# A hybrid decoder layer on one core: a plainer entry to the second feed-forward, held-back gate columns, a spread spatial-gating norm and later operand loads

## The chip, the cores and the metric

The kernel runs on one NeuronCore of a Trainium2 chip. The number that counts is device time in microseconds (us) of one execution. Before the change the median of three runs is 2202.64 us (2201.89 to 2203.19). The engines are named as the profile names them: PE is the matrix engine (TensorE), PEld its weight loads, DVE the vector engine, ACT the scalar engine, POOL GpSimd, SP the sync engine, whose queue issues the transfers spoken of here.

## The reference

One inference step of one decoder layer, for 1024 prompt tokens and 32 sample tokens (8 sequences of 4) that share the weights; D = 1024, feed-forward width 2816.

```python
h = layer_norm(ALPHA * x + 0.5 * swiglu(x, f1_w1, f1_w3, f1_w2), ln1_g, ln1_b)      # FFN-a
z = h @ w_in + b_in                       # 2304 for q, k, v; 1024 for u, v; 2048 for two gates
att = combine_groups(outs, lses)          # 3 groups of 4 heads, windowed and dilated attention
yb, vrows = sgu_branch(uv, sgu_ln_g, sgu_ln_b, sgu_ws, sgu_b)     # u * (tril(ws) @ LN(v) + b)
mix = (jax.nn.sigmoid(ga) * (att @ w_oa) + jax.nn.sigmoid(gb) * (yb @ w_ob)) @ w_out
h = layer_norm(ALPHA * h + mix, ln2_g, ln2_b)                                       # LN2
h = layer_norm(ALPHA * h + 0.5 * swiglu(h, f2_w1, f2_w3, f2_w2), ln3_g, ln3_b)      # FFN-b, LN3
```

Returned besides `h` are the key and value windows of both token kinds and `vrows`, the normalised v rows of the sample tokens (`svo` in the kernel). All is float32.

## The kernel before

**Layout.** Activations lie transposed, features on 128 partitions and the 1056 tokens along the free axis, cut into four column chunks of C = 264 (NC = 4). Every float32 operand is split into a rounded high part and a rest (`split`, L236 to L240: a cast on ACT at L238, a subtraction on DVE at L239), and a product takes three matmuls (`mm3`, L227): high by high, low by high, high by low. A dense 128-feature by 264-token product over 1024 inputs (`dense8`) is 24 such matmuls of 128x128 by 128x264. Feed-forward blocks go through a Strassen-like scheme (seven products of 24 matmuls, 168, for what takes 192 plainly); the blocks named in `PLAIN` can be done plainly by column chunk with `hidden8` (L405 to L419), which needs only the chunk's normalised columns.

**Stages.** FFN-a, the wide projection `w_in`, the mix (attention, spatial gating, gates, the three output products), then FFN-b. `gate8` (L944 to L956) computes one 128-feature block of z for one chunk on PE, evicts it on ACT (L954) and stores it to `zD` in DRAM (L955). `fetch_z` (L1102) loads a block of z back; `fetch_qkv` loads the three blocks that a step of attention needs.

**Mix.** `attend` (L1120 to L1233) runs six times, as a generator: per step V transposes (L1144), scores (L1164), mask and maximum on DVE (L1172), exponentials on ACT (L1176), turn transposes (L1187) copied by ACT (L1191), values (L1203), and a last transpose of maxima and sums (L1225), copied by DVE (L1227) and stored to `mlD` (L1229). The combination generator (L1235 to L1292) reads `mlD` in a [16, ...] form (L1247 to L1253), forms the weights of the three groups, stores them to `cD` (L1276), loads them broadcast over partitions (L1283) and scales the attention rows on DVE (L1288 to L1291). `sgu_norm` (L1402 to L1456) transposes the v blocks (L1433, copied at L1435), takes their statistics on DVE, the root on ACT and DVE (`rsqrt`, L628 to L634), and normalises with nine passes on ACT (L1447). `sgu_mix` (L1458 to L1487) makes `yb`. `mix` (L1489 to L1635) interleaves these with dense work: the last z blocks, then per output block n the product with w_ob (`local(n)`), which multiplies the gate tile `mt[n]` in place (L1505), and the product with w_oa, which is scaled by the gate tile `ta[n]` and added to it; the sum is split and feeds w_out.

**LN and FFN-b.** `norm` (L580 to L626) is a generator per chunk: sums of squares by ones-matmuls (L589), the root on ACT and DVE, a broadcast by matmul (L597), scaling on DVE (L608), affine on ACT (L616) or DVE (L613). In `ffn` (L641 to L721), block 0 of FFN-b is done chunk by chunk as LN2's chunks become ready; the spread sums (`s1`) that Strassen needs follow after chunk 3.

**What sets the order.** The file is a program of generators (`bg`, `mid`, `slow`) that dense work ticks by counted steps; a scheduler then sets each engine's order of instructions by simulated time and by the tile pools: 37 slots S, 8 weight tiles W, 6 mid tiles M, 2 raw tiles R, and the matmul banks mm (3) and ax (5). All transfers that are spoken of go through SP in the order written. An engine executes strictly in its order, so an instruction that waits holds all behind it.

Of the kernel before, what the change touches and what calls it, by code (L numbers as in the profile page):

```python
# [13 lines left out]
F32R = mybir.dt.float32r  # L14
AF = mybir.ActivationFunctionType
# [49 lines left out]
WARM = 2  # L65
FENCED = (mybir.EngineType.DVE, mybir.EngineType.Activation, mybir.EngineType.SP)
# [4 lines left out]
LAST = 4  # L71
EARLY = 6
# [7 lines left out]
class Trunk:  # L80
# [131 lines left out]
    def unit(self, src, n=D, slot=False, ahead=URGENT):  # L212
        new = self.S if slot else self.W
        with self.tc.high_priority(offset=ahead):
            raw = self.R([P, D])
            hi, lo = new([P, D], F32R), new([P, D], F32R)
            dma = self.nc.sync.dma_start(raw[:, :n], src[:, :n])
            self.split(hi[:, :n], lo[:, :n], raw[:, :n])
        self.fence[mybir.EngineType.SP] = dma.ins
# [362 lines left out]
    def norm(self, c, i, mode, Y, s):  # L582
# [7 lines left out]
        r, t = self.X([P, 3], "rs"), self.X([P, 3], "rt")  # L590
        self.rsqrt(r, t, pv, EPL)
# [35 lines left out]

    def rsqrt(self, r, t, v, eps):  # L628
# [12 lines left out]
    def ffn(self, w13, w2p, w2, i, mode, resid):  # L641
        nc, preps = self.nc, {}
        last = FB + NG * (KB // 2) - 1
# [27 lines left out]
        else:  # L671
# [3 lines left out]
            self.step(self.bg, 1)  # L675
            begin(1)
            for c in range(NC):
                self.drain(lns.pop(c))
                self.hidden8(units, 0, c)
                if c:  # L680
                    with self.chained():
                        next(preps[1], None)
            self.bg.append(s1)
# [5 lines left out]
        def ready(f):  # L689
            for _ in preps.pop(f):  # L690
                pass
            if f < last:
                begin(f + 1)

        def between(f, bg, slow=0):
            if f + 1 in preps:
                next(preps[f + 1], None)
# [8 lines left out]
        for f in range(1, FB):  # L706
# [5 lines left out]
            def after():  # L712
# [4 lines left out]
            self.hidden(f, after)  # L717
# [400 lines left out]
    def attend(self, i):  # L1118
# [19 lines left out]
        self.fetch_qkv(i + 1)  # L1138
# [77 lines left out]
        for t in range(6):  # L1216
# [4 lines left out]
            if t < 4:  # L1221
                scores(t)
            yield from self.pause(SPREAD)
# [12 lines left out]
    def combine(self, hp):  # L1236
# [3 lines left out]
        for g in range(3):  # L1240
            x = raw[:, g]
            for m in range(2):
                for h in range(2):
                    src = self.mlD[hp, g, m, h]
                    o = x[8 * h : 8 * h + 8, m]
                    if g == 0:
                        nc.sync.dma_start(o, src.rearrange("(a x) -> a x", a=8))  # L1247
                    elif g == 1:
                        nc.sync.dma_start(
                            o.rearrange("p (r b) -> p r b", r=4), src.rearrange("(r a b) -> a r b", r=4, a=8)  # L1250
                        )
                    else:
                        nc.sync.dma_start(  # L1253
                            o.rearrange("p (r b) -> p r b", r=16), src.rearrange("(r a b) -> a r b", r=16, a=8)
# [25 lines left out]
        cbs = [self.S([P, NP]) for _ in range(3)]  # L1280
        for g, cb in enumerate(cbs):
            for h in range(2):
                nc.sync.dma_start(cb[64 * h : 64 * h + 64], self.cD[hp, g, h].partition_broadcast(64))  # L1283
        yield from self.pause(3)
        for g, cb in enumerate(cbs):
            aT = self.attT.pop((hp, g))
# [113 lines left out]
    def sgu_norm(self):  # L1400
# [28 lines left out]
        for i in range(9):  # L1429
# [19 lines left out]
        v = self.M([NS, 512])  # L1449
        for op, k in ((ALU.mult, "sgu_ln_g"), (ALU.add, "sgu_ln_b")):  # L1450
            t = self.M([NS, 512])
            nc.sync.dma_start(t, a[k].partition_broadcast(NS))
            nc.vector.tensor_tensor(v, vn[4][:NS, 0] if op == ALU.mult else v, t, op=op)
        nc.sync.dma_start(a["svo"], v)
        self.vn = vn
# [32 lines left out]
    def mix(self):  # L1488
# [18 lines left out]
        def local(n):  # L1507
            wb = self.unit(a["wo"][n, :, 2 * P :], 4 * P)
# [12 lines left out]
        sgu = [self.sgu_norm()] + [self.sgu_mix(gg) for gg in range(4)]  # L1521
# [7 lines left out]
        for c in range(NC):  # L1529
# [4 lines left out]
            for n in units:  # L1534
                self.gate8(units[n], DENSE[n], c, AF.Identity, STEPS["tail"], 1)
        units = self.A = None
        while any(g in self.mid for g in sgu):
            self.step(self.mid, 1)
        def column_sums():
# [254 lines left out]
```

## Time and profile before

| what | value |
|---|---|
| median of three runs | 2202.64 us |
| profiled execution, its own time | 2200.98 us |
| its span (first to last instruction) | 2199.2 us |
| mean granted PE clock | 0.988 |
| PE, DVE, ACT, POOL busy in the span | 97%, 71%, 41%, 15% |
| chain that ended last | PE 81%, DMA 7%, DVE 7%, ACT 2% |

The profiled execution stands 1.66 us under the median, so a saving found in its trace is taken from the median without rescaling. Of the span, 1.8 us lie outside of it. The windows that matter are 1076 to 1330 us (attention beside spatial gating and gates), 1300 to 1400 (the end of attention, w_ob, w_oa and w_out), 1490 to 1550 (LN2 and the entry to FFN-b) and the last 20 us (LN3). In a row of a timeline stand the start, the length of the group, the engine, the line, the operation, out<-in and the count; in square brackets the idle time ahead of the group and what ended it. In a row of windows stand busy times and counts of PE, PEld, DVE, ACT and POOL, then the granted clock of PE, the share of the DMA engines and GB/s.

### The profile page before, as it was taken

The page shows a single profiled execution, that of the slowest core. Times are in us where ns is not written, and L with a number is a line of the kernel's source. Part 1 is how long each engine was busy: PE and PEld are TensorE (multiplying, and loading weights), DVE is VectorE, ACT ScalarE, POOL GpSimd, SP SyncE. Part 2 cuts the span into 40 slices and gives each one's busy share as a digit, 9 for nine tenths or more (in the row PEclk, how much of TensorE's full clock was granted, in tenths as well). Part 3 has the DMA queues.
Part 4 walks back from the last instruction along what each step waited for, and adds up shares of the span by engine and source line. Part 5 has one row for each costly group of instructions (what it writes and reads, how often), then busy time and mean ns, then how long its engine had stood idle before and what let it go on. Part 6 is the DMA issues. An engine that isn't in the chain of part 4 may idle for free.

```text
span 2199.2 us, 43234 instructions
## 1 busy us (share of the span) xinstructions
PE 2133.2 (97%) x17281; PEld 2092.9 (95%) x17281; DVE 1564.8 (71%) x2718; ACT 898.1 (41%) x1690; POOL 330.1 (15%) x238
## 2 busy tenths in 40 slices
PE   9999999999998999999989998998999999999997
PEld 8999999999998999999879897998999999999997
DVE  8777776656788725887674648778676776657787
ACT  5444444421225634344465354246444444322224
POOL 0432332200010022232000000000432332100000
PEclk9999999999999999999989999999999999999999
DMA  4435545598873325666854547513445545596751
GB/s 157 146 134 177 179 161 177 193 367 324 330 279 136 135 102 188 215 215 221 313 165 152 172 156 245 187 51 126 165 158 178 171 161 185 186 384 264 295 192 79
DMA packets 170553, 429.82 MB, mean 195 GB/s; under 512 B 24864, under 2 KB 61456, under 8 KB 167664
## 3 DMA queue, kind: packets, MB, share of 16 engines
q1 hardware_dynamic: 169920, 426.53, 55.3%
q8 instruction: 135, 2.21, 0.4%
q10 hardware_dynamic: 432, 0.54, 0.1%
q14 instruction: 66, 0.54, 0.1%
HBM read 305.97 MB, written 167.22 MB: 215 GB/s over the span
## 4 chain that ended last, share of the span: by engine, by line
PE 81%; DMA 7%; DVE 7%; ACT 2%; issue 1%; POOL 1%; SPq 1%; ACTq 0%; DVEq 0%; POOLq 0%
PE ax L227 43%; PE mm L227 35%; DMA M<-kv 4%; DVE W L239 1%; PE ax L1164 1%; DMA zD<-M 1%; DMA S<-zD 1%; PE ax L1203 1%; DVE S L239 1%; PE ax L1187 1%; DMA R<-wz 0%; DVE X L1346 0%; DVE S L608 0%; DVE X L1361 0%; DVE M L1345 0%
## 5 line engine op out<-in xcount | busy, mean ns | idle before, releaser
L227 PE MATMUL ax<-S,W 128*128 128x264 f32 x5472 | 716.2, 284 | 0.8 <-ACT S L994 0.5
L227 PE MATMUL mm<-S,W 128*128 128x264 f32 x5040 | 677.4, 289 | 25.8 <-DVE S L1505 9.3
L227 PEld LDWEIGHTS ax<-S,W 128*128 128x128 f32 x5472 | 685.6, 188 | 3.3 <-ACT S L994 1.5
L227 PEld LDWEIGHTS mm<-S,W 128*128 128x128 f32 x5040 | 641.6, 191 | 43.1 <-issue 10.7
L227 PE MATMUL ax<-S,S 128*128 128x264 f32 x3288 | 483.7, 285 | 2.9 <-DVE S L1003 2.8
L227 PEld LDWEIGHTS ax<-S,S 128*128 128x128 f32 x3288 | 434.2, 188 | 4.1 <-DVE S L1003 4.1
L227 PE MATMUL mm<-S,S 128*128 128x264 f32 x2496 | 388.4, 286 | 9.0 <-ACT S L238 4.0
L227 PEld LDWEIGHTS mm<-S,S 128*128 128x128 f32 x2496 | 337.7, 189 | 11.5 <-ACT S L238 4.4
L238 ACT CAST W<-R 128x256 fp32r<-128x256 f32 (+2 forms) x172 | 127.6, 759 | 316.8 <-PE mm L227 118.2
L369 POOL TENSOR_TENSOR Q<-R 128x512 f32<-128x512 f32 x50 | 72.1, 1443 | 793.1 <-DMA R<-w13b 217.1
L239 DVE TENSOR_TENSOR W<-R,W 128x256 fp32r<-128x256 f32 (+2 forms) x172 | 152.6, 891 | 28.2 <-ACT W L238 24.0
L238 ACT CAST W<-Q 128x1024 fp32r<-128x1024 f32 (+1 forms) x79 | 77.9, 986 | 217.1 <-POOL Q L370 91.7
L780 DVE SCALAR_TENSOR_TENSOR S<-ax,S 128x264 f32<-128x264 f32 x240 | 99.9, 431 | 69.6 <-PE ax L227 68.5
L444 DVE TENSOR_TENSOR S<-ax,M 128x264 f32<-128x264 f32 x84 | 33.7, 433 | 150.6 <-PE ax L227 150.6
L106 POOL CAST S<-ones 128x1 fp32r<-128x1 f32 x32 | 18.3, 594 | 745.5 <-PE mm L227 663.8
L239 DVE TENSOR_TENSOR S<-Q,S 128x1024 fp32r<-128x1024 f32 (+1 forms) x79 | 111.8, 1415 | 3.5 <-ACT S L238 3.3
L239 DVE TENSOR_TENSOR W<-Q,W 128x1024 fp32r<-128x1024 f32 (+1 forms) x79 | 92.0, 1164 | 24.5 <-ACT W L238 24.5
L238 ACT CAST S<-Q 128x1024 fp32r<-128x1024 f32 (+1 forms) x79 | 77.8, 985 | 74.1 <-PE ax L227 55.0
L238 ACT CAST S<-R 128x512 fp32r<-128x512 f32 (+1 forms) x65 | 44.6, 686 | 116.5 <-DMA sumsA<-S 42.6
L239 DVE TENSOR_TENSOR S<-S,M 128x528 fp32r<-128x528 f32 x72 | 85.6, 1189 | 2.1 <-ACT M L238 0.2
L370 POOL TENSOR_TENSOR Q<-Q,R 128x512 f32<-128x512 f32 x50 | 83.6, 1673 | 2.7
L377 POOL TENSOR_TENSOR Q<-R,Q 128x512 f32<-128x512 f32 x50 | 82.7, 1653 | 1.2
(199 smaller groups left out, 2063.3 us busy)
## 6 DMA issues: line engine op xcount, KB each, us to landing
ws<-st SPq DMA_DIRECT2D x144, 256.0 KB
S<-sumsA SPq DMA_DIRECT2D x63, 528.0 KB
S<-sumsB SPq DMA_DIRECT2D x63, 528.0 KB
M<-kv SPq DMA_DIRECT2D x96, 256.0 KB
sumsA<-M SPq DMA_DIRECT2D x90, 264.0 KB
sumsB<-M SPq DMA_DIRECT2D x90, 264.0 KB
R<-w13b SPq DMA_DIRECT2D x44, 512.0 KB
S<-zD SPq DMA_DIRECT2D x42, 528.0 KB
```

What stands on the lines that cost most here:

```text
L106: self.nc.gpsimd.tensor_copy(t[:, 0, :1] if len(shape) == 3 else t[:, :1], self.ones[:, :1])
L227: mm = lambda a, b, s, e: nc.tensor.matmul(o, a[:, cc], b, start=s, stop=e, skip_group_check=True)
L238: a = self.nc.scalar.copy(hi, src)
L239: b = self.nc.vector.tensor_tensor(lo, src, hi.bitcast(F32), op=ALU.subtract)
L369: tt(s12[:, lo], cd[:, lo], cd[:, hi], op=ALU.add)
L370: tt(s12[:, hi], s12[:, lo], ab[:, lo], op=ALU.subtract)
L377: tt(s34[:, hi], ab[:, hi], s12[:, hi], op=ALU.subtract)
L444: go(one, 5, False, lambda x: tt(h[:, x, 1], one[x], p7[:, x], op=ALU.add))
L780: nc.vector.scalar_tensor_tensor(y(x, r, e), bank[x], HALF, y(x, r, e), op0=ALU.mult, op1=ALU.add)
L1164: nc.tensor.matmul(pS[h][:, r, :nk], q[e, i * P : (i + 1) * P], k[e, k0 : k0 + nk], start=True, stop=True)
L1187: nc.tensor.transpose(pT[r][:, h, o], s[:, r, h, o], self.ident)
L1203: nc.tensor.matmul(pv[0][e, (i % 4) * P : (i % 4 + 1) * P], V[:, i - (nb - 1) + b, e], sT[:, r, h, b * P : b * P + P], start=b == 0, stop= ...
```

## The change

Five things are changed; line numbers move by some 12 to 60 in the new file.

1. FFN-b starts with two plain blocks, 0 and 19, each done chunk by chunk behind LN2 (FFN-a keeps one); the spread sums `s1` are queued ahead of the last chunk. Block 19 is left out of the later Strassen blocks.
2. The last gate units, three now (four before), are computed for chunks 0 to 2 only; their chunk 3 is done by `beside` after the w_oa blocks 2, 4 and 5. All eight w_ob blocks stand before the end of attention (six before). Their weights, and those of w_oa, take one W tile (`narrow`), and `ta` is fetched three blocks ahead.
3. `sgu_norm` takes its root on DVE (`rsqrt_dve`: an integer start and three Newton steps, eleven small instructions) and pauses two steps between transposes; the stored sample rows are a generator of their own at the end of the list.
4. LN2's last chunk and LN3's third chunk take their root on DVE; one Silu activation on a single column follows LN2's third chunk.
5. `fetch_qkv` of the next step moves from the start of a step to its `t == 3`; the combination reads `mlD` of group 0 with one transfer, and loads the three broadcast tiles one after another.

```diff
@@ narrow (new)
+    def narrow(self, src, n):
+        with self.tc.high_priority(offset=URGENT):
+            raw = self.R([P, D])
+            both = self.W([P, D], F32R)
+            hi, lo = both[:, :n], both[:, n : 2 * n]
+            dma = self.nc.sync.dma_start(raw[:, :n], src)
+            self.split(hi, lo, raw[:, :n])
...
@@ norm
+        if c == NC - 1 and i == 1 or c == NC - 2 and mode == "out":
+            self.rsqrt_dve(r, t, self.X([P, 3], "rx", 1), pv, EPL)
+        else:
+            self.rsqrt(r, t, pv, EPL)
+        if i == 1 and c == NC - 2:
+            nc.scalar.activation(self.X([P, 2], "warm", 1)[:, :1], r[:, :1], AF.Silu)
...
+    def rsqrt_dve(self, r, t, x, v, eps):
+        nc = self.nc
+        tt = nc.vector.scalar_tensor_tensor
+        nc.vector.tensor_scalar(x, v, eps, None, op0=ALU.add)
+        nc.vector.tensor_scalar(r.bitcast(I32), x.bitcast(I32), -0.5, MAGIC, op0=ALU.mult, op1=ALU.add)
+        for _ in range(3):
+            nc.vector.tensor_tensor(t, x, r, op=ALU.mult)
+            tt(t, t, -0.5, r, op0=ALU.mult, op1=ALU.mult)
+            self.chain = tt(r, t, 1.5, r, op0=ALU.add, op1=ALU.mult).ins
@@ ffn
+        plain = PLAIN[: 1 if i == 0 else 2]
+        blocks = [f for f in range(FB) if f not in plain] + [FB + g for g in range(NG * (KB // 2))]
...
+            lead = [units] + [[self.unit(w13[f, x]) for x in range(2)] for f in plain[1:]]
             begin(1)
             for c in range(NC):
                 self.drain(lns.pop(c))
-                self.hidden8(units, 0, c)
...
-            self.bg.append(s1)
+                if c == NC - 1:
+                    self.bg.append(s1)
+                    self.step(self.bg, 2)
+                for f, u in zip(plain, lead):
+                    self.hidden8(u, f, c)
...
@@ attend
-        self.fetch_qkv(i + 1)
+        follower = i + 1
...
+            if t == 3:
+                self.fetch_qkv(follower)
             yield from self.pause(SPREAD)
@@ combine
+            if g == 0:
+                nc.sync.dma_start(x, src.rearrange("m h (a x) -> (h a) m x", a=8))
...
+        load(0)
+        load(1)
         yield from self.pause(3)
-        for g, cb in enumerate(cbs):
+        for g in range(3):
+            load(g + 2)
...
@@ sgu_norm
-            yield
+            yield from self.pause(2)
...
-        self.rsqrt(rs[:, 0], rs[:, 1], mv[:, :, 1], EPS)
+        self.rsqrt_dve(rs[:, 0], rs[:, 1], mv[:, :, 1], mv[:, :, 1], EPS)
...
@@ mix
-            wb = self.unit(a["wo"][n, :, 2 * P :], 4 * P)
+            wb = self.narrow(a["wo"][n, :, 2 * P :], 4 * P)
...
-            for n in units:
-                self.gate8(units[n], DENSE[n], c, AF.Identity, STEPS["tail"], 1)
-        units = self.A = None
+            if c < NC - 1:
+                for n in units:
+                    self.gate8(units[n], DENSE[n], c, AF.Identity, STEPS["tail"], 1)
...
+        def beside(n):
+            m = DENSE[n] - 26
+            p = self.mm_tile()[:, :C]
+            self.dense8(p, units.pop(n), NC - 1)
+            with self.urgent():
+                nc.scalar.activation(ta[m][:, -C:], p, AF.Identity, bias=self.bin(DENSE[n]))
...
-        for n in range(EARLY):
+        for n in range(KB):
             local(n)
-        ta = [self.fetch_z(26 + n) for n in range(2)]
+        self.yb = None
+        ta = [fetch_gate(n) for n in range(3)]
...
-            wa = self.unit(a["wo"][n], 2 * P)
-            if n + 2 < KB:
-                ta.append(self.fetch_z(28 + n))
-            if n < KB - EARLY:
-                local(EARLY + n)
+            wa = self.narrow(a["wo"][n, :, : 2 * P], 2 * P)
+            if n + 3 < KB:
+                ta.append(fetch_gate(n + 3))
...
+            if n in BESIDE:
+                beside(BESIDE[n])
```

Where the order of the engines moves is shown at three places. The first is ACT at the spatial-gating norm, beside the second step of attention: the table load and root of `sgu_norm`, the nine normalising passes, and the exponentials of the attention step. Before:

```order
L630 ACT_TABLE_LOAD
L630 ACTIVATE X_13274<-X_12957,eps_163 128x9
L1145 COPY Q_13366<-ax_13367 128x512
L1210 COPY S_12932<-ax_13231 128x512
L1145 COPY Q_13366<-ax_13373 128x512
L1447 ACTIVATE S_12952<-S_12952,X_13274 128x512 x2
L1447 ACTIVATE S_12953<-S_12953,X_13274 128x512 x2
L1447 ACTIVATE S_12954<-S_12954,X_13274 128x512 x2
L1447 ACTIVATE S_12955<-S_12955,X_13274 128x512 x2
L1447 ACTIVATE S_12956<-S_12956,X_13274 32x512
L1176 ACT_TABLE_LOAD
L1176 ACTIVATE S_13415,X_13413<-S_13415,X_13413 128x128
```

After, where L1212 are the exponentials, L990 the evictions of `gate8`, L1227 the copies of the turn and L1489 the nine passes:

```order
L1212 ACTIVATE S_13390,X_13388<-S_13390,X_13388 128x128
L1212 ACTIVATE S_13390,X_13388<-S_13390,X_13388 128x256
L990 ACTIVATE M_13639<-mm_13614,cols 128x264
L1227 COPY S_13413<-ax_13406 128x512
L1227 COPY S_13413<-ax_13405 128x2x128
L1489 ACTIVATE S_12942<-S_12942,X_13434 128x512 x2
L1489 ACTIVATE S_12943<-S_12943,X_13434 128x512 x2
L1489 ACTIVATE S_12944<-S_12944,X_13434 128x512 x2
L1489 ACTIVATE S_12945<-S_12945,X_13434 128x512 x2
L1489 ACTIVATE S_12946<-S_12946,X_13434 32x512
L990 ACTIVATE M_13680<-mm_13655,cols 128x264
L1212 ACTIVATE S_13416,X_13388<-S_13416,X_13388 128x128
```

The two table loads are gone, and the nine passes stand behind the first turn of the step instead of ahead of its first exponentials.

The second place is SP at the end of attention. In the names, zD is z in DRAM, mlD and cD the tables of the combination; L1102 before and L1138 after are `fetch_z`, here the tiles `mt[4]` and following. Before:

```order
L1102 DMA S_15245<-zD_8669 128x1056
L1102 DMA S_15247<-zD_8670 128x1056
L1229 DMA mlD<-X_15237 32x128
L1247 DMA S_15282<-mlD 8x128 x4
L1249 DMA S_15282<-mlD 8x4x32 x4
L1253 DMA S_15282<-mlD 8x16x8 x4
```

After:

```order
L1311 DMA cD<-S_15276 16x128 x3
L1321 DMA S_15306<-cD 64x1024 x2
L1321 DMA S_15309<-cD 64x1024
L1138 DMA S_15312<-zD_8666 128x1056
L1138 DMA S_15314<-zD_8667 128x1056
L1138 DMA S_15322<-zD_8668 128x1056
L1321 DMA S_15309<-cD 64x1024
L1321 DMA S_15344<-cD 64x1024
L1138 DMA S_15412<-zD_8669 128x1056
```

Blocks zD_8669 and zD_8670 (`mt[4]`, `mt[5]` before; the numbering of zD differs by three between the files, so that these are zD_8666 and zD_8667 after) stood ahead of the store to `mlD` and stand behind the store to `cD` now.

The third place is ACT at the entry to FFN-b, where L415 and L428 evict a gate of block 0, L616 and L635 are LN2's affine passes. Before, with two changes of table and back around the root of chunk 3 (L630):

```order
L328 CAST S_17454<-S_17413 128x1056
L415 ACT_TABLE_LOAD
L415 ACTIVATE M_17638<-mm_17588 128x264
L238 CAST S_17150<-S_16387 128x1056
L328 CAST S_17488<-S_17456 128x1056
L328 CAST S_17522<-S_17411 128x1056
L328 CAST S_17554<-S_17490 128x1056
L630 ACT_TABLE_LOAD
L630 ACTIVATE X_17571<-ax_17567,eps_165 128x3
L415 ACT_TABLE_LOAD
L415 ACTIVATE M_17714<-mm_17664 128x264
```

After, where the loads are gone from this stretch (the one that remains, at L610, stands ten rows ahead of the first of these):

```order
L341 CAST S_17426<-S_17385 128x1056
L428 ACTIVATE M_17630<-mm_17580 128x264
L251 CAST W_17576<-R_17570 128x1024
L251 CAST S_17122<-S_16360 128x1056
L341 CAST S_17460<-S_17428 128x1056
L341 CAST S_17494<-S_17383 128x1056
L341 CAST S_17526<-S_17462 128x1056
L428 ACTIVATE M_17706<-mm_17656 128x264
L428 ACTIVATE M_17760<-mm_17710 128x264
```

The first evictions of block 0 and block 19 follow one another, with no root of chunk 3 on ACT between them.

More of the change, by code (lines that the diff above doesn't have):

```diff
@@ L704, in load @@
                     loads.popleft()()
-        for f in range(1, FB):
+        for f in blocks[: FB - len(plain)]:
             ready(f)
@@ L710, in ffn, with step @@
             count = iter(range(1, 8))
-            def after():
+            def step():
                 between(f, STEPS["strassen"])
@@ L715, in after @@
                     load(min(HEAD, 2 + 4 * next(count)))
-            self.hidden(f, after)
+            self.hidden(f, step)
             del self.L[f]
```

82 lines of the change are left out of this document (47 added, 35 removed).

## The prediction

> **What bounds the kernel now.** I read the windows first, to see where PE is not busy.
>
> ```profile
> 1100.00:1150.00 50.00, 42.52 (x356) 36.84 (x355) 35.30 (x96) 33.12 (x81) 0.00 (x0) 0.90 0.55 168
> 1150.00:1200.00 50.00, 48.45 (x379) 43.65 (x379) 26.00 (x86) 27.98 (x83) 0.00 (x0) 0.93 0.48 157
> ...
> 1300.00:1350.00 50.00, 44.31 (x345) 42.35 (x345) 34.96 (x84) 19.21 (x40) 0.00 (x0) 0.93 0.61 195
> 1350.00:1400.00 50.00, 43.08 (x321) 40.76 (x321) 45.16 (x70) 19.86 (x23) 2.66 (x6) 0.97 0.79 284
> ...
> 1500.00:1550.00 50.00, 45.11 (x347) 44.17 (x347) 41.13 (x55) 25.53 (x39) 8.13 (x6) 0.93 0.37 125
> 1550.00:1600.00 50.00, 50.00 (x413) 50.00 (x412) 33.52 (x49) 22.02 (x38) 16.83 (x12) 1.00 0.50 171
> ```
>
> The last row is a window in which PE is the bound: 413 matmuls in 50 us, 0.121 us each; there only fewer matmuls help. The others lose time twice, by idle PE and by a granted clock under 1. I count a window's loss as 50 minus busy, plus busy times (1 minus clock). 1100 to 1200 loses 7.5 + 4.3 + 1.6 + 3.4 = 16.7 us; 1300 to 1400 loses 5.7 + 3.1 + 6.9 + 1.3 = 17.0 us. For 1500 to 1550 the count does it: 413 - 347 = 66 matmuls, 8.0 us. These 42 us are nearly all that the change can win. The list of PE's waits says for whom PE waits (total, times, longest):
>
> ```profile
> PE ax L1187 <- ACT S L1176: 10.0, 4, 5.9
> PE mm L227 <- DVE S L1505: 9.3, 9, 3.2
> PE mm L227 <- ACT S L238: 8.8, 3, 4.0
> PE mm L227 <- ACT M L415: 2.7, 3, 1.9
> ...
> PE ax L1144 <- DMA S<-zD: 1.3, 1, 1.3
> ```
>
> The first is attention behind ACT, the second w_ob and w_oa behind DVE's gate products, the third and fourth mostly the entry to FFN-b; the last is part 3's. The timeline shows each.
>
> **Part 1: plain entry to FFN-b.** Block 19 takes 192 matmuls instead of 168: 24 by 0.121 = **+2.9 us**, certain, since PE is the bound in this stage. What it can win is the entry's loss (the first row is part 4's):
>
> ```profile
> 1336.15 4.19 PE L227 MATMUL mm<-S,W 128*128 128x264 f32 x21 [3.18 <-DVE S L1505]
> ...
> 1493.94 2.83 PE L227 MATMUL mm<-S,S 128*128 128x264 f32 x21 [1.87 <-ACT M L415]
> ...
> 1504.15 0.73 PE L597 MATMUL ax<-ident,X 128*128 128x128 f32 x6
> ...
> 1511.91 0.81 PE L227 MATMUL mm<-S,S 128*128 128x264 f32 x2 [4.02 <-ACT S L238]
> 1512.52 1.74 PE L227 MATMUL mm<-S,W 128*128 128x264 f32 x7
> ```
> ```profile
> 1492.20 1.28 ACT L415 ACT_TABLE_LOAD   x1
> ...
> 1497.79 1.28 ACT L630 ACT_TABLE_LOAD   x1
> ...
> 1499.37 1.28 ACT L415 ACT_TABLE_LOAD   x1
> ```
>
> The 1.87 us wait is an eviction behind the first of these table loads; the warm-up activation moves that load ahead, and the root of chunk 3 on DVE takes the other two away. The 4.02 us wait is for LN2's chunk 3, whose split on ACT is late, and the matmuls behind it run at 1.74/7 = 0.25 us each. After the change, about 130 dense matmuls (15.7 us) lie on PE between the broadcast of chunk 3's root and the first matmul that reads chunk 3; before, 24 (2.9 us). From that broadcast to the first matmul PE took from 1504.15 to 1511.91, 7.8 us, and 15.7 us of cover is twice that. Loss taken away: 8.0 + 1.9 = 9.9 us. Late next is block 19's second weight: its rest comes from a raw tile that is cast and subtracted when ACT is full of LN2. As nearest row I take the first wait above, behind ACT in the same crowd, and leave 1.9 us (bounds 0, all hidden, and 5.9, the longest wait of the list). Net of it −8.0, with the matmuls **−5.1 us** (−7.0 to −1.1).
>
> [...] The 0.25 us behind the 4.02 us wait agree with half clock. [...]
>
> **Part 2: spatial gating.** Before, ACT does the root and nine passes in one piece, and PE waits for the exponentials behind them:
>
> ```profile
> 1119.93 1.28 ACT L630 ACT_TABLE_LOAD   x1
> ...
> 1124.34 6.46 ACT L1447 ACTIVATE S<-S,X 128x512 f32<-128x512 f32 x9 [0.27 <-DVE X L1443]
> 1130.82 1.28 ACT L1176 ACT_TABLE_LOAD   x1
> 1132.12 0.40 ACT L1176 ACTIVATE S<-S,X 128x128 f32<-128x128 f32 x1
> ```
> ```profile
> 2182.95 0.17 DVE L631 RECIPROCAL X<-X 128x3 f32<-128x3 f32 x1
> ...
> 2184.08 0.16 DVE L634 SCALAR_TENSOR_TENSOR X<-X,X 128x3 f32<-128x3 f32 x1
> ```
> ```profile
> 1134.98 1.54 PE L1187 MATMUL ax<-ident,S 128*128 128x128 f32 x6 [5.88 <-ACT S L1176]
> ...
> 1139.51 3.74 PE L227 MATMUL mm<-S,W 128*128 128x264 f32 x22
> ...
> 1149.81 0.88 PE L1187 MATMUL ax<-ident,S 128*128 128x128 f32 x6 [1.15 <-ACT S L1176]
> 1151.86 2.73 PE L1164 MATMUL ax<-S,S 64*128 64x128 f32 x8 [1.18 <-DVE M L1483]
> ```
>
> The root on DVE is eleven instructions. Of the four that DVE does now, the row in the middle shows those of LN3, 0.16 us each; with other work between they start up to 0.4 us apart. At 0.2 us eleven are 2.2 us, on an engine that was busy 35.30 of 50 us: hidden, as nobody but the nine passes waits for it. Two table loads, 2.6 us, go from ACT. The nine passes still take 6.46 us in one piece, but they stand behind a turn's copies, with some 60 dense matmuls (7.3 us) on PE ahead of the next turn. What is late next: three turns, score groups and values follow with no dense work between, since all three matmul banks wait for an eviction on ACT. By the old waits at the same places (1.15, 1.18, and half of 5.88) I leave 5.3 us idle and half of the 7.7 us lost to clock. From 16.7 us that is 9.2 left, −7.5; because pauses push the gating back toward the end of attention I take **−6.0 us** (−12 to 0).
>
> **Part 3: operands later.** `fetch_qkv` moves from a step's start to its fourth turn, on SP behind what stands there:
>
> ```profile
> 1124.93 6.97 SPq L1330 DMA_DIRECT2D M<-kv  x6
> ...
> 1327.11 1.05 SPq L1102 DMA_DIRECT2D S<-zD  x2
> ...
> 1333.85 1.08 ACT L1513 ACTIVATE S<-S 128x1056 f32<-128x1056 f32 x1 [2.29 <-DMA S<-zD]
> ```
>
> Six slabs of the sample caches hold the queue 7 us, and a block of z took 6.7 us from issue to its first reader. Between the moved loads and the first V transposes PE has 6 to 9 us of work in the new order. So each of five steps may wait between 0 and 6.7 us; what waits behind a V transpose is all of PE. PE waited only once for such a load before, 1.3 us. I take 0.8 us each, **+4.0 us** (0 to 33). It buys slots S for other tiles, whose worth no row shows: nothing.
>
> **Part 4: gate columns held back, w_ob first.** The 72 matmuls of three units' chunk 3 and the order of w_ob leave 78 fewer dense matmuls ahead of the end of attention: 9.4 us earlier, and the work comes back behind it, where PE idled (3.18 us at 1336.15, and then):
>
> ```profile
> 1309.29 0.27 PE L1225 MATMUL ax<-ident,X 128*32 128x128 f32 x1
> ...
> 1342.60 1.01 PE L227 MATMUL mm<-S,W 128*128 128x264 f32 x3 [2.26 <-ACT S L238]
> ...
> 1383.42 35.68 PE L227 MATMUL mm<-S,W 128*128 128x264 f32 x288 [1.35 <-DVE S L1505]
> ```
>
> Call t0 = 1309.3 the last transpose of attention. Before, w_out begins at t0 + 74; from then on PE has no wait. DVE is the bound in between (45.16 of 50 us busy). After, w_ob block 4 needs `mt[4]`, whose load was issued ahead of t0 and now is behind the combination:
>
> ```profile
> 1304.17 1.58 SPq L1102 DMA_DIRECT2D S<-zD  x2
> ...
> 1309.90 0.32 SPq L1229 DMA_DIRECT2D mlD<-X  x1
> ...
> 1322.60 1.26 SPq L1276 DMA_DIRECT2D cD<-S  x3
> 1324.02 3.04 SPq L1283 DMA_DIRECT2D S<-cD  x5
> ```
>
> Issued near t0 + 15 and 6.7 us in flight, it lands at t0 + 22, while PE's other work, 60 matmuls and the first three chunks of that block (36), 11.6 us, ends with what stands between near t0 + 14: a new wait of 7 to 9 us, which also delays DVE's products. That puts w_out at t0 + 76 to t0 + 79 by my count of DVE's work (the gate additions and splits of eight blocks do not change). Against 74 this is +2 to +5, less the 9.4: **−5.9 us** (−9.4, no wait, to 0). At t0 itself the last turns of step 5 have no dense work between them, as the banks are held by w_ob blocks whose gate tile is not there: **+2.5 us** (0 to 5.9, the longest such wait).
>
> **Part 5: the tail.** LN3's third chunk does its root on DVE, where before ACT shared it (the rows at 2182.95 and 2184.08 above). Seven more small instructions, 1.4 us at 0.2, on the engine that ends the kernel; less some that fill its short idle spells, **+1.2 us** (0 to 2).
>
> **Sum.** −5.1 − 6.0 + 4.0 − 5.9 + 2.5 + 1.2 = −9.3 us; from the profiled 2200.98 that is 2191.7, and from the median, 1.66 above it, **2193.3 us**. Fewer transfers by SP are counted at nothing: between 1305.75 and 1309.90, rows above, its queue issues nothing.
>
> **Rivals.** (a) *The late operands decide, slower.* Without its +4.0 the sum is −13.3; at 3.6 us for each of five steps it is +4.7, and slower from there on. At 4.5 us each, two thirds of the flight of 6.7, it is +9.2: 2211.8 us. For it speaks the queue's 7 us of slabs; against it that PE has 6 to 9 us of other work there. (b) *The mix gains nothing.* DVE stays the bound after t0, the banks stall PE as ACT did before, and only the entry and the tail count: −5.1 + 1.2 = −3.9, 2198.7 us. For it speaks the 45.16 of 50; against it the 5.88 us wait whose cause is taken away. (c) *The entry does not change.* Block 19's weights come as late as chunk 3 did: the entry keeps its loss and pays +2.9; the mix gives −5.4 and the tail +1.2: −1.3, 2201.3 us. For it speaks that ACT was the releaser both times. (d) *Both halves go better than counted:* no waits for operands and no stall at t0, −9.3 − 4.0 − 2.5 = −15.8, 2186.8 us.
>
> **How the numbers follow.** A difference under 0.2% (4.4 us) cannot be told from none. I give the forecast 0.49 (0.47 of it beyond 4.4 us), (d) 0.10, (b) 0.15 (half same, half faster, a little slower), (c) 0.07 (same), (a) 0.19. Faster: 0.47 + 0.10 + 0.07 = 0.64. Same: 0.02 + 0.07 + 0.07 = 0.16. Slower: 0.19 + 0.01 = 0.20. The range leaves out the far ends of (a) and of (d), each about 1 in 10: 2181 to 2208 us. The forecast's own range is 2187 to 2199.
>
> **What would show it.** In the changed profile: no idle time over 2 us on PE between LN2 and Strassen block 1, and granted clock near 1 there; no table load beside `sgu_norm`, and waits behind the exponentials of 6 us or less in all; a wait of 7 to 9 us on w_ob's fifth block shortly after the last transpose of attention; w_out begun some 8 us earlier than 1383.42; and in the last 20 us one more us. I am wrong if V transposes wait for `S<-zD` by more than 3 us a step, or if the stretch from w_oa to w_out grows by more than 5 us.

## The result: no change in time

The changed kernel takes 2204.1 us in the median of 14 runs (2198.1 to 2209.2); the kernel before, in 14 runs, 2203.4 us. The ratio is 1.0001 with a 95% interval of 0.9992 to 1.0011. The forecast was 9.3 us less. The profiled execution after has a span of 2203.5 us; like the one before (2199.2) it is a single draw out of a scatter of several us, which the last section speaks of. Where only traces are compared, I therefore count between three marks that both kernels have: the V transposes of attention's step 0 (mark A, 1074.51 before, 1076.37 after), the last transpose of attention (t0, 1309.29 and 1306.41) and LN2's third broadcast, that of its chunk 2 (mark B, 1481.63 and 1489.27; the recorded expectations call it the second).

### The profile page after: what moved, and what is told of

The parts are those of the page before. It is cut to its first block, busy times and chain, and to the rows that moved or that the text cites. A ratio compares the mean times of both kernels' runs of the same rounds, so it can differ in the third digit from the quotient of the medians.

```text
span 2203.5 us, 43277 instructions
## 1 busy us (share of the span) xinstructions
PE 2136.6 (97%) x17305; PEld 2097.4 (95%) x17305; DVE 1554.4 (71%) x2731; ACT 888.5 (40%) x1678; POOL 322.2 (15%) x234
## 4 chain that ended last, share of the span: by engine, by line
PE 82%; DMA 8%; DVE 6%; ACT 1%; issue 1%; POOL 1%; SPq 0%; ACTq 0%; DVEq 0%; POOLq 0%
PE ax L240 43%; PE mm L240 36%; DMA M<-kv 4%; DMA S<-zD 1%; DVE W L252 1%; PE ax L1200 1%; DMA R<-wz 1%; DVE M L1398 1%; PE ax L1239 0%; DVE X L1403 0%; PE ax L1223 0%; DVE M L1387 0%; ACT W L251 0%; DVE S L252 0%; DVE X L1388 0%
## 5 line engine op out<-in xcount | busy, mean ns | idle before, releaser
L240 PE MATMUL mm<-S,W 128*128 128x264 f32 x5208 | 698.3, 290 | 28.8 <-DVE S L1551 12.9
L240 PE MATMUL ax<-S,W 128*128 128x264 f32 x5400 | 708.1, 285 | 1.4 <-ACT S L1030 1.0
L240 PEld LDWEIGHTS mm<-S,W 128*128 128x128 f32 x5208 | 663.9, 192 | 44.9 <-DVE S L1551 15.1
L240 PEld LDWEIGHTS ax<-S,W 128*128 128x128 f32 x5400 | 677.5, 188 | 4.4 <-ACT S L1030 2.6
L240 PE MATMUL ax<-S,S 128*128 128x264 f32 x3240 | 476.7, 284 | 3.4 <-DVE S L1039 3.3
L240 PEld LDWEIGHTS ax<-S,S 128*128 128x128 f32 x3240 | 427.8, 188 | 4.6 <-DVE S L1039 4.6
L240 PE MATMUL mm<-S,S 128*128 128x264 f32 x2472 | 384.1, 285 | 2.6 <-DVE S L252 2.2
L240 PEld LDWEIGHTS mm<-S,S 128*128 128x128 f32 x2472 | 334.2, 188 | 4.3 <-DVE S L252 2.4
L251 ACT CAST W<-R 128x1024 fp32r<-128x1024 f32 (+3 forms) x173 | 128.8, 761 | 320.3 <-PE mm L240 142.5
L252 DVE TENSOR_TENSOR W<-R,W 128x1024 fp32r<-128x1024 f32 (+3 forms) x173 | 148.9, 865 | 30.1 <-ACT W L251 29.8
```

The source lines that it names most:

```text
L240: mm = lambda a, b, s, e: nc.tensor.matmul(o, a[:, cc], b, start=s, stop=e, skip_group_check=True)
L251: a = self.nc.scalar.copy(hi, src)
L252: b = self.nc.vector.tensor_tensor(lo, src, hi.bitcast(F32), op=ALU.subtract)
```

## The profile after

PE's waits, as the list of the changed kernel gives them (total, times, longest; L240 is the dense matmul, L1551 the gate product, L1223 the turn, L1180 the V transposes, L616 the norm's broadcast):

```profile
PE mm L240 <- DVE S L1551: 12.9, 8, 8.4
PE ax L1223 <- ACT S L1212: 10.9, 5, 4.3
...
PE ax L1180 <- DMA S<-zD: 4.3, 3, 1.9
...
PE ax L616 <- DVE X L663: 2.7, 1, 2.7
...
PE ax L616 <- DVE X L655: 1.8, 1, 1.8
```

The waits for LN2's chunk 3 and for the evictions of block 0 are gone; the wait for the gate products has grown from 9.3 to 12.9 us with one of 8.4. The wait for the exponentials has not shrunk in all (10.0 before, 10.9 now), though its longest piece has (5.9 before, 4.3 now). The timeline of PE shows the large one and the new entry to FFN-b:

```profile
1082.91 8.62 PE L240 MATMUL mm<-S,W 128*128 128x264 f32 x46 [2.97 <-ACT M L990]
...
1329.54 14.29 PE L240 MATMUL mm<-S,W 128*128 128x264 f32 x96 [8.38 <-DVE S L1551]
...
1379.76 19.04 PE L240 MATMUL mm<-S,W 128*128 128x264 f32 x150 [1.03 <-DVE S L1551]
...
1498.59 4.63 PE L240 MATMUL mm<-S,W 128*128 128x264 f32 x36 [1.35 <-DVE W L252]
```

The large wait, of 8.38 us, is for the products with `mt[4]`. On SP's queue the loads of that tile and the next (three `S<-zD` at 1323.52) stand behind the last store to `mlD`, the store to `cD` and the first broadcasts from it; on VectorE the scaling of the attention rows (L1330) waits 6.80 us for its broadcast, and behind it the products (L1551) wait another 0.81 us for the tile:

```profile
1307.03 0.31 SPq L1267 DMA_DIRECT2D mlD<-X  x1
...
1319.45 1.30 SPq L1311 DMA_DIRECT2D cD<-S  x3
1321.75 1.73 SPq L1321 DMA_DIRECT2D S<-cD  x3
1323.52 1.53 SPq L1138 DMA_DIRECT2D S<-zD  x3
```
```profile
1326.61 1.23 DVE L1330 TENSOR_TENSOR S<-S,S 128x1024 f32<-128x1024 f32 x1 [6.80 <-DMA S<-cD]
...
1329.05 1.11 DVE L1551 TENSOR_TENSOR S<-S,mm 128x264 f32<-128x264 f32 x3 [0.81 <-DMA S<-zD]
```

The windows between the marks say where the time is. First mark A to t0, of before and of the changed kernel, then the same for the dense matmuls alone (busy time, count, clock):

```profile
1074.51:1309.29 234.78, 218.17 (x1794) 194.99 (x1795) 133.70 (x411) 126.31 (x351) 0.00 (x0) 0.96 0.57 182
...
1074.51:1309.29 234.78, 142.73 (x1026) 0.96 0.57 182
```
```profile
1076.37:1306.41 230.04, 210.19 (x1715) 187.82 (x1716) 131.14 (x404) 120.71 (x342) 0.00 (x0) 0.96 0.53 175
...
1076.37:1306.41 230.04, 133.32 (x948) 0.96 0.53 175
```

Then t0 to mark B:

```profile
1309.29:1481.63 172.34, 159.73 (x1249) 156.10 (x1247) 134.63 (x225) 64.36 (x102) 7.38 (x14) 0.97 0.45 157
```
```profile
1306.41:1489.27 182.86, 168.52 (x1328) 165.55 (x1325) 138.10 (x239) 68.16 (x110) 6.65 (x14) 0.96 0.46 156
```

Ahead of t0, 78 dense matmuls are gone (1026 to 948), 9.4 us at 0.121, and the stretch is only 4.7 us shorter: PE's idle time there rose from 16.6 to 19.9 us. Behind t0 these 78 are paid in full: the stretch is 10.5 us longer, and PE's idle time rose from 12.6 to 14.3. From mark A to B that is 407.1 and 412.9 us. Behind mark B the changed kernel takes 709.9 us to the end of its last vector instruction (2199.20), before 713.2 (to 2194.83): that is the entry to FFN-b and the tail together, −3.3.

## The experiments

Theory A: the mix's gain went into the wait for `mt[4]`, which now is loaded behind the combination's transfers. Theory B: behind t0 VectorE is the bound, whatever matrix work there is. C, D and F come up as the runs ask for them. The experiments were timed in three groups, each with runs of the kernel before beside it (medians 2203.2, 2204.7 and 2203.6 us), so it is the ratios that are compared; a gain or loss in us beside a ratio is that ratio's share of 2203 us.

**Gate tiles early.** Three gate tiles per chunk instead of two, so that `mt[4]` and `mt[5]` stand ahead of the last store to mlD.

```diff
-                    for n in range(2 * c - 2, 2 * c):
+                    for n in range(3 * c - 3, min(3 * c, 6)):
```

> The changed kernel, with one thing other: the gate tiles mt[0] to mt[5] are fetched three per chunk (0 to 2, then 3 to 5), so that mt[4] and mt[5] stand ahead of the last store to mlD again, as before the change. Theory A (late tiles: the gain of the mix went into the 8.4 us wait for mt[4] and the slow clock behind it): that wait falls under 2 us, VectorE multiplies w_ob's products while the combination's transfers are in flight, w_out begins 6 to 9 us earlier than t0 + 85, and the time is about 2204 - 7 = 2197 us (2194 to 2200). Theory B (VectorE is the bound after t0, whatever matrix work is there): the wait is gone, but w_out begins at t0 + 83 to t0 + 85 all the same and the time stays within 2 us of 2204.

Measured: 2195.3 us, ratio to before 0.9965 (0.9952 to 0.9978), some 8 us less than the change, from which it differs in this line alone. The loads now stand ahead of the last store to `mlD`. The size of the gain is what theory A gave; its picture was not. PE still has one wait of that kind, and as long:

```profile
1291.05 1.52 SPq L1138 DMA_DIRECT2D S<-zD  x3
...
1301.48 0.32 SPq L1267 DMA_DIRECT2D mlD<-X  x1
```
```profile
1300.87 0.27 PE L1263 MATMUL ax<-ident,X 128*32 128x128 f32 x1
...
1328.90 11.75 PE L240 MATMUL mm<-S,W 128*128 128x264 f32 x72 [8.61 <-DVE S L1551]
```
```profile
1327.16 1.23 DVE L1332 TENSOR_TENSOR S<-S,S 128x1024 f32<-128x1024 f32 x1 [4.77 <-DMA S<-cD]
1328.42 1.11 DVE L1551 TENSOR_TENSOR S<-S,mm 128x264 f32<-128x264 f32 x3
```
```profile
1072.33:1300.87 228.54, 135.02 (x989) 0.97 0.57 184
```

What ends PE's wait here is no gate tile: VectorE waits 4.77 us for a broadcast of the combination, and the products, which stand behind that scaling in its order, follow without a wait of their own. What differs from the change is the count ahead of t0: 989 dense matmuls (948 in the change) in a stretch of 228.5 us (230.0). With their tiles there, 41 more matmuls of w_ob (5.0 us) run ahead of t0, and the stretch from t0 to B is 175.9 us instead of 182.9.

**The entry alone.** Of the change only the second plain block, the spread sums queued ahead of the last chunk, and LN2's last root with the early activation:

```diff
+        plain = PLAIN[: 1 if i == 0 else 2]
+        if c == NC - 1 and i == 1:
+            self.rsqrt_dve(r, t, self.X([P, 3], "rx", 1), pv, EPL)
...
```

> The kernel before, with only the second plain block at the entry to FFN-b and LN2's last root on VectorE with the early Silu activation; mix, attention, gating and LN3 as before. If the entry is worth what the two traces show between LN2 and the tail (4.5 us), the time is about 2199 us (2197 to 2201) and PE has no wait over 2 us between LN2 and the first Strassen block. If the entry's gain is only noise of the clock, it is 2203 to 2206 us, by 24 matmuls more.

Measured: 2198.1 us, ratio 0.9976 (0.9963 to 0.9990), −5.3 us. The entry is worth what the prediction said (−5.1).

**The mix alone.** The change without those lines (and LN3 as before):

```diff
-        if c == NC - 1 and i == 1 or c == NC - 2 and mode == "out":
-            self.rsqrt_dve(r, t, self.X([P, 3], "rx", 1), pv, EPL)
...
-        plain = PLAIN[: 1 if i == 0 else 2]
```

> The changed kernel without the entry: FFN-b, LN2 and LN3 as before, all of the mix as changed. If the mix costs what the entry and the tail leave over (2204.1 + 4.5 - 1.3), about 2207 us (2205 to 2210), slower than before. If the mix is neutral and the loss lies elsewhere (FFN-b's later blocks, the tail), 2202 to 2204 us.

Measured: 2202.9 us, ratio 0.9998 (0.9983 to 1.0013): inside the second range, that of a neutral mix. Its reason, a loss elsewhere, does not hold beside the entry's −5.3. The mix as a whole neither gains nor loses by more than some 3 us. Its stretch from t0 to B is 182.8 us, as in the change, so that stretch is reproducible.

**Held-back columns in the gap.** The 72 matmuls stand where PE waited for `mt[4]`:

```diff
-BESIDE = {2: 13, 4: 14, 5: 15}
+BESIDE = {}
...
             local(n)
+            if n == 3:
+                for m in units:
+                    self.gate8(units[m], DENSE[m], NC - 1, AF.Identity, 0, 0)
+                units = self.A = None
```

> The changed kernel, but the 72 held-back matmuls (chunk 3 of the last three gate units) are done between the w_ob blocks 3 and 4, where PE waited 8.4 us for mt[4], and not beside w_oa. Theory A (a wait is all that is lost there): the 8.7 us of work fill the 8.4 us wait, and the time falls to about 2197 us (2194 to 2200). Theory B (VectorE is the bound after t0): w_out begins as late as it does, at t0 + 83 to t0 + 86, the waits come back between the w_oa blocks, and the time is 2202 to 2206 us.

Measured: 2200.1 us, ratio 0.9984 (0.9970 to 0.9998), just above theory A's range and below theory B's. The wait at that place fell from 8.4 to 2.9 us, yet t0 to B took 182.6 us, as before the edit:

```profile
1333.61 11.60 PE L240 MATMUL mm<-S,W 128*128 128x264 f32 x77 [2.94 <-DVE S L1551]
```
```profile
1361.79:1371.79 10.00, 6.89 (x45) 5.86 (x46) 8.80 (x14) 6.25 (x6) 0.00 (x0) 1.00 0.68 255
1371.79:1381.79 10.00, 6.41 (x47) 5.61 (x45) 10.00 (x16) 4.18 (x4) 0.00 (x0) 1.00 0.47 151
```

The wait moved: between the w_oa blocks PE now idles 3.1 and 3.6 us of 10 while VectorE is busy 8.80 and 10.00. Filling PE's wait is of no use when VectorE idles through it as well and has to make up its work later. What is left of the wait, 2.94 us, again ends with VectorE, which waited 5.36 us for a broadcast of the combination. So theory A, that PE's wait itself is the loss, does not hold in the trace. The profiled execution is 5.5 us shorter than the change's (spans of 2198.0 and 2203.5), but 3.6 of these lie ahead of mark A, where the order of the engines is the same.

**Column sums on GpSimd.** Theory B taken at its word: 6 us off VectorE's list.

```diff
-                nc.vector.tensor_reduce(
-                    wr[:, q], raw.rearrange("p (k x) -> p k x", x=P), axis=AX.X, op=ALU.add
-                )
+                v, w = raw.rearrange("p (k x) -> p k x", x=P), P // 2
+                while w > 1:
+                    nc.gpsimd.tensor_tensor(v[:, :, :w], v[:, :, :w], v[:, :, w : 2 * w], op=ALU.add)
+                    w //= 2
+                nc.gpsimd.tensor_tensor(wr[:, q], v[:, :, 0], v[:, :, 1], op=ALU.add)
```

> The changed kernel with one thing other: the five column sums of w_out (1.2 us each on VectorE, 6.1 us in all, four of them behind t0) are done on GpSimd, which is idle in the mix, as halving additions. Theory B (behind t0 VectorE's work sets when w_out begins): w_out begins 4 to 6 us earlier than t0 + 85 though PE still waits 8 us for mt[4], and the time falls to 2198 to 2201 us. Theory A (the wait for mt[4] is what is lost): the stretch from t0 to LN2's second broadcast (182.9 us) stays within 2 us and the time at 2202 to 2206 us.

Measured: 2205.2 us, ratio 1.0000 (0.9989 to 1.0011), t0 to B 181.8 us: nothing gained. All five sums, 6.1 us, are gone from VectorE, yet from t0 to B it is busy only 3.6 us less (134.5 against 138.1): beside GpSimd's additions some of its operations took longer, a 128x256 subtraction at 1347.71 for one 0.98 us instead of 0.43. By theory B w_out should have begun 3.6 us sooner after t0; it began 0.8 sooner. As far as this smaller relief can tell, VectorE's load alone does not set the stretch either. Between t0 + 10 and t0 + 20 both kernels show the same, PE busy half the time and VectorE a third of it, and from t0 + 30 PE is nearly full for two windows:

```profile
1316.41:1326.41 10.00, 4.75 (x40) 4.54 (x38) 3.31 (x9) 3.02 (x4) 0.00 (x0) 0.91 0.46 111
1326.41:1336.41 10.00, 6.88 (x37) 6.88 (x38) 7.05 (x12) 2.01 (x4) 0.00 (x0) 0.58 1.05 316
1336.41:1346.41 10.00, 9.59 (x79) 9.36 (x78) 8.41 (x15) 5.78 (x8) 0.00 (x0) 1.00 0.91 351
1346.41:1356.41 10.00, 10.00 (x83) 9.99 (x83) 6.67 (x15) 1.84 (x4) 0.00 (x0) 1.00 0.44 133
```

These are windows of the changed kernel. Before, the two windows from t0 + 10 were:

```profile
1319.29:1329.29 10.00, 10.00 (x85) 10.00 (x84) 7.13 (x19) 1.12 (x3) 0.00 (x0) 1.00 0.55 152
1329.29:1339.29 10.00, 6.82 (x45) 6.60 (x44) 9.09 (x13) 5.33 (x7) 0.00 (x0) 0.83 1.03 309
```

Neither engine alone is the bound behind t0: both stand still in the combination's flight, and afterwards now one, now the other is full.

**Gating alone.** Of the change only `sgu_norm`:

```diff
-            yield
+            yield from self.pause(2)
...
-        self.rsqrt(rs[:, 0], rs[:, 1], mv[:, :, 1], EPS)
+        self.rsqrt_dve(rs[:, 0], rs[:, 1], mv[:, :, 1], mv[:, :, 1], EPS)
```

> The kernel before, with only the spatial-gating norm changed (root on VectorE, pauses, the sample rows as a generator of their own). By the prediction's term 2196.6 us (-6.0). By the two profiled windows from 1100 to 1200 (16.7 us lost before, 14.1 after) about 2200 us (-2.6). If the gating's waits only change place, 2202 to 2205 us. In the profile the two table loads beside the norm are gone and PE's wait of 5.9 us for the exponentials falls to under 4.5.

Measured: 2195.0 us, ratio 0.9952 (0.9939 to 0.9965), −10.6 us, more than any of the three readings. The two profiled executions are 6.6 us apart. Of these, 3.9 lie between mark A and t0 (230.9 us with the same 1026 dense matmuls; t0 to B is 172.4) and 3.8 ahead of mark A, where no instruction's place has changed: those are chance. The longest wait for the exponentials is 4.3 us, though their sum hardly fell (9.7 us). How much of the −10.6 belongs to the norm is therefore open.

**Early tiles, old tail.** The first experiment, with LN3's third root on ACT:

```diff
-        if c == NC - 1 and i == 1 or c == NC - 2 and mode == "out":
+        if c == NC - 1 and i == 1:
```

> The changed kernel with the gate tiles fetched early (as in e1_gates_early) and LN3's third root on ACT again. The tail's term says -1.3 against e1_gates_early's 2195.3: 2194 us (2191 to 2197), with one wait of PE for the broadcast in the last 15 us instead of two.

Measured: 2191.4 us, ratio 0.9942 (0.9926 to 0.9959). Of the two waits for the broadcast (2.7 and 1.8 us) one is left, of 2.3. The step from the first experiment (0.9965) is no better known than its interval.

**The same with the sums on GpSimd.** The edit is that of the fifth experiment, on this kernel.

> e7_early_tail with the column sums on GpSimd as well. Theory B: VectorE's products fill the combination's flight and 6 us are off its list, so 4 to 6 us less than e7_early_tail, 2188 to 2191 us. Theory A: with mt[4] early nothing more is lost to VectorE, and it is within 2 us of e7_early_tail.

Measured: 2196.0 us, ratio 0.9959 (0.9947 to 0.9972), not faster than without. Here VectorE is busy 131.8 us from t0 to B instead of 133.8, as it again slowed beside GpSimd (a 128x1024 subtraction took 2.08 us, alone 1.22). Theory B finds no support, but with a relief of 2.0 us it is hardly tested.

**Entry and gating.** Both of the two parts that gain, nothing else.

```diff
+        plain = PLAIN[: 1 if i == 0 else 2]
...
-        self.rsqrt(rs[:, 0], rs[:, 1], mv[:, :, 1], EPS)
+        self.rsqrt_dve(rs[:, 0], rs[:, 1], mv[:, :, 1], mv[:, :, 1], EPS)
```

> The kernel before with the entry to FFN-b (as in e2_head_alone) and the spatial-gating norm (as in e6_gating_alone), and nothing else of the change. If the two gains add, 2203.5 - 5.2 - 9.7 = about 2188.5 us (2186 to 2192). Theory C (part of e6's gain is luck of the clock, as profiled stretches before any difference vary by some us): 2192 to 2196 us.

Measured: 2194.2 us, ratio 0.9953 (0.9940 to 0.9965), −10.4 us, inside the range of theory C: the two singly add up to 15.9. Values that lie in all three intervals are about −4 and −8.

**Late operands added.** With them go the combination's transfers as changed.

```diff
-        self.fetch_qkv(i + 1)
+        follower = i + 1
...
+            if t == 3:
+                self.fetch_qkv(follower)
```

> e9_head_gating with the operands of attention fetched at the fourth turn and the combination's transfers as changed. Theory D (what eats the two gains is the gate columns held back: they were filler for attention's waits and come back behind t0 in full): within 2 us of e9_head_gating. Rival (a) of the prediction (late operands decide): 4 to 10 us more than it, with more than 1.5 us of waiting for S<-zD at each V transpose.

Measured: 2192.8 us, ratio 0.9949 (0.9937 to 0.9961), within 1 us of the one without. The list has the waits, three and 5.1 us in all, where the kernel without had one of 0.9; they cost nothing that shows.

```profile
PE ax L1169 <- DMA S<-zD: 5.1, 3, 2.4
```

**Held-back columns added.** The other half of the mix (with the narrow weights), on the entry and gating:

```diff
-LAST = 4
-EARLY = 6
+LAST = 3
+BESIDE = {2: 13, 4: 14, 5: 15}
...
-        for n in range(EARLY):
+        for n in range(KB):
             local(n)
```

> e9_head_gating with part 4 alone: three gate units, their chunk 3 beside w_oa, all of w_ob ahead, narrow weights. Theory D: 8 to 12 us more than e9_head_gating (2197 to 2200), the stretch from the V transposes of step 0 to t0 as long as in e9 though 78 dense matmuls are gone from it, and that from t0 to LN2's second broadcast near 182.8 instead of 172.4 us. Rival (a): within 3 us of e9_head_gating.

Measured: 2200.0 us, ratio 0.9983 (0.9972 to 0.9993): 6 us more than without (the intervals of the two do not meet). Of the entry and gating alone, then with the columns, mark A to t0 (dense matmuls) and t0 to B:

```profile
1073.42:1307.07 233.65, 142.00 (x1026) 0.97 0.57 183
...
1307.07:1479.63 172.56, 161.13 (x1250) 158.11 (x1248) 134.99 (x225) 66.16 (x104) 6.65 (x14) 0.95 0.46 157
```
```profile
1076.15:1305.37 229.22, 133.06 (x948) 0.95 0.54 176
...
1305.37:1489.15 183.78, 166.87 (x1327) 164.00 (x1325) 138.59 (x239) 68.25 (x110) 6.65 (x14) 0.96 0.45 156
```

−4.4 us ahead of t0 for 9.4 us of work, +11.2 behind it: this part is what ate the gains. In this kernel too the loads of `mt[4]` and its followers stand behind the store to `cD`.

**Early tiles, columns not held back.** The seventh experiment, with chunk 3 of all gate units done ahead:

```diff
-            if c < NC - 1:
-                for n in units:
-                    self.gate8(units[n], DENSE[n], c, AF.Identity, STEPS["tail"], 1)
+            for n in units:
+                self.gate8(units[n], DENSE[n], c, AF.Identity, STEPS["tail"], 1)
+        units = self.A = None
```

> e7_early_tail (gate tiles early, LN3's root on ACT) with chunk 3 of the last three gate units done ahead, not held back. Theory D: ahead of t0 the 72 matmuls fill waits and cost 0 to 3 us, behind it 8.7 us go: 2191.4 - 6 = 2185 us (2182 to 2188). Theory F (with mt[4] early, held-back columns fill PE's waits between the w_oa blocks as they were meant to): within 2 us of 2191.4, or above.

Measured: 2190.3 us, ratio 0.9938 (0.9924 to 0.9952), within 1.1 us of the seventh. The seventh experiment, then this one, mark A to t0 (dense matmuls) and t0 to B:

```profile
1074.59:1305.91 231.32, 135.04 (x989) 0.96 0.56 182
...
1305.91:1477.71 171.80, 160.73 (x1286) 157.79 (x1284) 133.82 (x223) 67.60 (x108) 6.67 (x14) 0.98 0.46 157
```
```profile
1072.71:1311.95 239.24, 143.59 (x1027) 0.94 0.56 185
...
1311.95:1479.57 167.62, 157.95 (x1248) 154.00 (x1246) 132.15 (x221) 63.91 (x100) 7.46 (x14) 0.99 0.43 152
```

So, with the tiles early, holding the columns back neither costs nor gains by more than the intervals; theory D, that the columns were free filler, falls with it: here they lengthen the stretch to t0 by 7.9 us and shorten the rest by 4.2. PE's longest wait for a gate product fell from 7.3 to 1.2 us, and the time did not follow: that wait is not what counts. What cost the change most of its gain is the late tiles that came with the held columns. This is the kernel with the lowest median, 0.6% under the one before, though not apart from the seventh. Late tiles without held columns were not run.

**All traces side by side.** Each row puts together the traces of one kind (us, lowest to highest):

| dense columns, gate tiles | traces | A to t0 | t0 to B | A to B | PE idle, A to B |
|---|---|---|---|---|---|
| not held, tiles as before | before, entry, gating, both | 230.9 to 234.8 | 172.3 to 174.5 | 403.2 to 408.8 | 23.5 to 30.0 |
| held, tiles late | change, mix, gap, sums, held columns added | 224.6 to 231.2 | 181.8 to 183.8 | 407.4 to 413.0 | 33.1 to 34.8 |
| held, tiles early | first, seventh, eighth experiment | 228.5 to 234.0 | 171.8 to 175.9 | 403.1 to 409.8 | 28.8 to 30.2 |
| not held, tiles early | the last experiment | 239.2 | 167.6 | 406.9 | 27.4 |
| not held, operands late | late operands added | 227.4 | 177.7 | 405.1 | 26.3 |

The dense work from A to B is the same in all. Behind t0 and in PE's idle time the rows of late tiles and of early tiles do not overlap; ahead of t0 they do, and there a difference between two single traces is no result. Behind mark B the traces fall into three narrow kinds: 713.2 to 714.7 us without the new entry, 707.4 to 708.9 with it, 709.3 to 709.9 with the new tail as well.

## Why the prediction was wrong

- **The entry, −5.1: right.** Alone −5.3. The two waits are gone; at block 19's first use PE waits 1.35 us, where 1.9 was allowed, and the window from 1500 to 1550 is full (50.00 of 50 us). Behind mark B the traces put it at some −6 (708.1 against 714.1 us in the mean).
- **The gating, −6.0: right in kind, its size open.** Alone it measured −10.6 with an interval of 2.9 to each side; beside the entry it added 5.1 to the entry's −5.3. The nine passes do stand behind the turn's copies, and the longest wait is 4.3 us instead of 5.9. But the sign that the prediction named, waits behind the exponentials of 6 us or less in all, did not come: 9.7 alone, 10.9 in the change.
- **Late operands, +4.0: too dear.** The waits came, three of them and none over 2.4 us, but the time did not move with them: −0.9 us (0.9949 against 0.9953), with an interval of some 4 us to each side. Rival (a), 3.6 us or more for each of five steps, was far off.
- **The gate columns and w_ob, −5.9, and the stall at t0, +2.5: the step that failed.** The new wait for `mt[4]` was forecast at 7 to 9 us and is 8.38. The mistake is in what the text made of it: "That puts w_out at t0 + 76 to t0 + 79". It began at t0 + 83 (78 matmuls into the group at 1379.76), so at 1389.7 and not some 8 us earlier than 1383.42. The prediction took VectorE as the bound behind t0 and its work as unchanged, so that matmuls brought there would be free; but with the tiles late VectorE too stood still (3.31 us busy of 10, before 7.13), waiting for the combination with no product to do meanwhile, and the 9.4 us were paid in full. And ahead of t0 it took 78 matmuls fewer as 9.4 us earlier; 4.4 is what the columns alone gave in the pair of traces, as PE waits for attention there instead. Together the part came to +6.6 (3.6 to each side) where −3.4 stood: some 10 us, about as much as the whole miss. Fetching the tiles early took some 8 us of it back.
- **The tail, +1.2: right in the trace.** PE's two waits in the last 15 us, 0.98 and 2.30 us before, are 1.82 and 2.68 now, and behind mark B the kernels with the new tail take 1.6 us more in the mean. The instructions of the root start up to 0.7 us apart, where 0.4 was read from the trace before.
- Of the rivals, (b), "the mix gains nothing", came nearest; its reason, VectorE as the bound, found no support: with 3.6 us less on VectorE behind t0 the time did not change. The measured 2204.1 lies above its 2198.7, and above what the parts add up to: entry and gating −10.4, operands −0.9, columns +6.6, tail +1.2 make −3.5 against +0.2 with an interval of 2. The parts' own intervals (2.8) allow that; whether operands and columns together cost more than singly was not settled.

## What to carry to other kernels

A wait priced on one engine has to be priced on the engine behind it too: what a late load costs is what all engines leave undone meanwhile. Neither filling PE's hole nor relieving VectorE shortened the stretch behind t0 (182.6 and 181.8 us against 182.9), while issuing the same loads ahead of attention's last store did (175.9). When work is moved from one stretch to another, look at which transfers change place with it: in every kernel here that holds the columns back and fetches the tiles as before, attention's last stores stand ahead of two loads in the queue. Whether the missing work or the tile slots put them there was not tested. And a change made of several parts that gain and one that loses shows as no change; run the parts alone before believing in any of them.

## What the runs showed of the hardware

The same instructions at the same places do not take the same time. Up to mark A PE, ACT, GpSimd and SP's queue have the same instructions in the same order in all fourteen traces, by operation, kind of tile and shape, yet mark A falls between 1068.1 and 1078.1 us; and a single execution of the kernel before took between 2196 and 2211 us. Both PE's idle time and its clock differ there: ahead of mark A PE idled 17.3 us before, 17.5 us in the changed kernel and 12.8 us in the mix alone; its mean granted clock up to 660 us was 0.99 before and 1.00 in the changed kernel, and from there to 1070 us 1.00 and 0.99.

The clock shows best at one place behind mark A. Ten of the traces have a wait of 2.93 to 3.00 us ahead of the same 46 matmuls. In five these took 5.84 or 5.85 us, in five 7.24 to 8.62. Before:

```profile
1081.02 5.85 PE L227 MATMUL mm<-S,W 128*128 128x264 f32 x46 [2.93 <-ACT M L954]
```

In the changed kernel (the row at 1082.91 above) they took 8.62 us behind 2.97; the mean granted clock during them was 1.00 before and 0.64 after. Elsewhere in the profile before, the granted clock was 0.50 over the seven matmuls at 1512.52, shortly behind the wait of 4.02 us, and 0.63 over the 21 at 1336.15, behind one of 3.18 us. Behind a wait of 3 us, then, the same 46 matmuls took up to 2.8 us more in one execution than in the next; what decides on the clock was not shown. In these runs trace differences of under some 5 us ahead of t0 between two single profiles are not results.
